# Moving two vector operations of each expert behind later weight splits in a mixture-of-experts kernel

## The chip, the cores and the metric

The kernel runs on one core of a Trainium2 chip. The figure is the device time of one execution in microseconds (us). TensorE (PE) multiplies matrices, VectorE (DVE) and ScalarE (ACT) work element by element, GpSimd (POOL) issues the gathers and scatters, SyncE (SP) issues the loads. Each engine works through its own queue in order; an instruction that waits holds up everything behind it on that engine.

## The reference

The program is a chain of a gated-linear-attention layer, a mixture-of-experts layer, a Fourier and attention layer and a recurrent layer on 512 tokens of width 1024. The change lies in the mixture of experts: 32 experts, each token goes to four of them.

```python
def expert_block(args):
    xblk, e = args
    gu = xblk @ w_gu[e] + b_gu[e]              # 1024 x 2048
    gate, up = jnp.split(gu, 2, axis=-1)
    gate = jnp.minimum(gate, SWIGLU_LIMIT)
    up = jnp.clip(up, -SWIGLU_LIMIT, SWIGLU_LIMIT)
    act = (up + 1.0) * gate * jax.nn.sigmoid(SWIGLU_ALPHA * gate)
    return act @ w_down[e] + b_down[e]         # 1024 x 1024
...
y = jnp.zeros((n_tok + 1, D_MODEL), yb.dtype).at[buf_tok].add(yb * buf_w[:, None].astype(yb.dtype))
```

## The kernel before

Every float32 product is made of three matmuls on rounded halves: a high part `hi` (a rounded copy, made by ACT, line 147) and a low part `lo` (source minus `hi`, made by DVE, line 148). Making the pair is called a split here. `W.get` loads one 1 MB block of weights (128 x 2048 values, tile `raw`, nine buffers) and splits it into `whi` and `wlo` (four pairs of buffers). So the split of a block can begin only when PE has finished with the block four before it, and SP may load a block only when the split nine before it is over.

One expert has twelve such blocks: eight of `w_gu` (called G0 to G7 here) and four of `w_down` (D0 to D3). Per pass of the loop over experts, the program's text has these steps: `gate_up(e)` (96 matmuls of 96 rows by 512 columns into `pgu`, four banks of PSUM, one buffer, and four more for the bias), `swiglu(e)`, `down(e - 1)` (48 matmuls into `pd`, one buffer, behind two for the bias), then `turn` of expert e's activation. In the middle of `gate_up(e)` the gathered tokens of expert e + 1 are turned (`pxT`, `xTh`, `xTl`), and in every fourth expert up to the 25th index tables for later experts are made (`tables`: matmuls `ptab` and small DVE operations).

The names on the path, in both programs:

- `g` and `u`: DVE reads `pgu` twice (lines 1166 and 1168 before), ACT applies Silu to `g` (L1167), DVE makes `u` of both (L1169). `pgu` is free for the next expert once the two reads are over.
- `paT`, `aTh`, `aTl`: PE turns `u` (L1128), ACT and DVE split it (L1134, L1135). `aTh`/`aTl` have one buffer, which the matmuls of `down` read.
- `y`: DVE scales `pd` (L1186) when `down` is over; POOL scatters it into the result (L1187).

What stands where on an engine is decided by a scheduler that reorders the instructions of the text by a model of their costs, unless an edge is given by hand. `tc.issue_after(ins)` gives such edges: each instruction in the block is placed behind `ins` on `ins`'s engine and waits for nothing more.

Of the kernel before, what the change touches and what calls it, by code (L numbers as in the profile page):

```python
# [9 lines left out]
F32 = mybir.dt.float32  # L10
# [5 lines left out]
OP = mybir.AluOpType  # L16
# [4 lines left out]
D = 1024  # L21
# [5 lines left out]
NE = 32  # L27
TK, XK, BK = 1, 5, 4

AH, SH, HN = 9, 7, 3  # L30
# [112 lines left out]
def split(S, hi, lo, src):  # L143
    if S.any:
        S.nc.any.tensor_copy(hi, src)
    else:
        S.nc.scalar.copy(hi, src)  # L147
    S.nc.vector.tensor_tensor(lo, src, hi.bitcast(F32), op=OP.subtract)  # L148


def mm3(S, ps, lh, ll, rh, rl, start, stop):
# [6 lines left out]
class Weights:  # L158
# [45 lines left out]
    def get(self, view, shape):  # L204
        S = self.S
        rv = self.early.pop(0) if self.early else self.load(view, shape)
        n = int(np.prod(shape[1:]))
        hi, lo = self.pair()
        hv, lv = hi[:shape[0], :n], lo[:shape[0], :n]
        if len(shape) == 3:  # L210
            hv = hv.rearrange("p (a b) -> p a b", a=shape[1])
            lv = lv.rearrange("p (a b) -> p a b", a=shape[1])
        split(S, hv, lv, rv)
        return hv, lv
# [742 lines left out]
def tables(S, pl, bank, b):  # L957

    nc = S.nc
    es = slice(b * 4, b * 4 + 4)  # L960
    oh = pl.tile([128, NT, 4, SLOTS], BF, name="oh", tag="oh", bufs=1)
    iota = S.k[:, None, K_IOTA:K_IOTA + SLOTS].to_broadcast([128, 4, SLOTS])
    for i in range(NT):
        nc.vector.tensor_tensor(oh[:, i], iota, S.pos[:, i, es, None].to_broadcast([128, 4, SLOTS]), op=OP.is_equal)
    p = bank("ptab")
    for e in range(4):
        for i in range(NT):
            nc.tensor.matmul(p[:SLOTS, e * 6:e * 6 + 6], oh[:, i, e, :], S.V[:, i, b * 4 + e, :], start=i == 0, stop=i == NT - 1)
    sl = pl.tile([SLOTS, 4, 6], F32, name="sl", tag="sl", bufs=2)
    nc.vector.tensor_copy(sl, p[:SLOTS, 0:24].rearrange("p (e c) -> p e c", e=4))  # L970
    t = pl.tile([SLOTS, 4, 4], F32, name="tsl", tag="tsl", bufs=2)
    tok, sct = t[:, :, 0], t[:, :, 1]
    nc.vector.tensor_tensor(tok, sl[:, :, 0], sl[:, :, 1], op=OP.add)
    nc.vector.tensor_copy(S.gi[:, es], tok)

    nc.vector.scalar_tensor_tensor(sct, sl[:, :, 2], S.k[:SLOTS, K_NSLOT:K_NSLOT + 1], tok, op0=OP.mult, op1=OP.add)
    nc.vector.tensor_scalar(S.si[:, es], sct, S.k[:SLOTS, K_SLOT:K_SLOT + 1], None, op0=OP.add)
    nc.vector.tensor_tensor(sct, sl[:, :, 3], sl[:, :, 4], op=OP.add)
    nc.vector.tensor_tensor(S.wt[:, es], sct, sl[:, :, 5], op=OP.add)
# [114 lines left out]
def phase_b(S):  # L1094
    nc, tc, I = S.nc, S.tc, S.I
    mm = nc.tensor.matmul
    with ExitStack() as bx:
# [4 lines left out]
        W = Weights(S, bx, 2048, 9, "b_w", (2, 3, 0, 1, 4, 5, 8, 6, 7))  # L1102
# [11 lines left out]
        xg, xT, aT, ac = {}, {}, {}, {}  # L1114

        def gather(e, gi=None):
            xg[e] = pl.tile([SLOTS, D], F32, name="xg", tag="xg", bufs=2)
            gi = S.gi[:, e:e + 1] if gi is None else gi
            S.gathered = nc.gpsimd.indirect_dma_start(out=xg[e], out_offset=None, in_=S.h2d,
                                         in_offset=bass.IndirectOffsetOnAxis(ap=gi, axis=0)).ins  # L1120

        def turn(src, dst, e, name, bufs, scale=1.0):
            dst[e] = [pl.tile([128, KT, SLOTS], F32R, name=name + n, tag=name + n, bufs=bufs) for n in "hl"]
            for h in range(2):
                p = bank("p" + name)
                for k in range(4):
                    kk = h * 4 + k
                    nc.tensor.transpose(p[:, k * SLOTS:(k + 1) * SLOTS], src[:, kk * 128:(kk + 1) * 128], S.ident[:SLOTS, :SLOTS])  # L1128
                hi, lo = [t[:, h * 4:h * 4 + 4, :] for t in dst[e]]
                p = p[:, :4 * SLOTS].rearrange("p (k t) -> p k t", k=4)  # L1130
                if scale == 1.0:
                    split(S, hi, lo, p)
                else:
                    nc.scalar.mul(hi, p, scale)  # L1134
                    nc.vector.scalar_tensor_tensor(lo, p, scale, hi.bitcast(F32), op0=OP.mult, op1=OP.subtract)  # L1135

        def bias(p, e, c, b, start, stop):
            lhs = sel[:, b // 3, e:e + 1].to_broadcast([128, SLOTS])
            mm(p[:, c * 512:(c + 1) * 512], lhs, bt[:, b % 3 * 512:(b % 3 + 1) * 512], start=start, stop=stop)  # L1139
# [7 lines left out]
        def gate_up(e, between):  # L1147
            p = ps.tile([SLOTS, 2048], F32, name="pgu", tag="gu", bufs=1)
            xh, xl = xT.pop(e)
            for k in range(KT):  # L1150
                if k in between:
                    between[k]()
                wh, wl = held.pop(0) if held else W.get(I["w_gu"][0, e, k * 128:(k + 1) * 128, :], [128, 2048])
                for a, w in ((xh, wh), (xh, wl), (xl, wh)):
                    for c in range(4):
                        mm(p[:, c * 512:(c + 1) * 512], a[:, k, :], w[:, c * 512:(c + 1) * 512],  # L1156
                           start=k == 0 and w is wh and a is xh, stop=False)
            for c in range(4):
                bias(p, e, c, c, False, True)
            return p  # L1160

        def swiglu(e, p):

            g = pl.tile([SLOTS, D], F32, name="g", tag="g", bufs=1)
            u = pl.tile([SLOTS, D], F32, name="u", tag="u", bufs=1)
            nc.vector.tensor_scalar(g, p[:, 0:D], 7.0, None, op0=OP.min)  # L1166
            nc.scalar.activation(g, g, AF.Silu, scale=ALPHA)  # L1167
            nc.vector.tensor_scalar(u, p[:, D:2 * D], 7.0, -7.0, op0=OP.min, op1=OP.max)  # L1168
            nc.vector.scalar_tensor_tensor(u, u, 1.0, g, op0=OP.add, op1=OP.mult)  # L1169
            return u  # L1170

        def down(e):
            p = ps.tile([SLOTS, D], F32, name="pd", tag="dn", bufs=1)
            for c in range(2):
                bias(p, e, c, 4 + c, True, False)
            ah, al = aT.pop(e)
            for k0 in range(0, KT, 2):
                wh, wl = W.get(I["w_down"][0, e, k0 * 128:(k0 + 2) * 128, :].rearrange("(k p) c -> p k c", p=128),
                               [128, 2, D])
                for k in range(2):  # L1180
                    for a, w in ((ah, wh), (ah, wl), (al, wh)):
                        for c in range(2):
                            mm(p[:, c * 512:(c + 1) * 512], a[:, k0 + k, :], w[:, k, c * 512:(c + 1) * 512],  # L1183
                               start=False, stop=k0 + k == KT - 1 and a is al)
            y = pl.tile([SLOTS, D], F32, name="y", tag="y", bufs=2)
            nc.vector.scalar_tensor_tensor(y, p, S.wt[:, e:e + 1], S.g2b, op0=OP.mult, op1=OP.mult)  # L1186
            nc.gpsimd.indirect_dma_start(out=S.ydr, out_offset=bass.IndirectOffsetOnAxis(ap=S.si[:, e:e + 1], axis=0),  # L1187
                                         in_=y, in_offset=None, compute_op=OP.add)

# [20 lines left out]
        held = [W.get(I["w_gu"][0, 0, k * 128:(k + 1) * 128, :], [128, 2048]) for k in range(HN)]  # L1210
# [3 lines left out]
        for e in range(NE + 1):  # L1214
            if e < NE:
                between = {BK: biases} if e == 0 else {}
                if e % 4 == 0 and e // 4 + 1 < NE // 4:
                    between[TK] = lambda: tables(S, pl, bank, e // 4 + 1)
                if e + 1 < NE:
                    between[XK] = lambda: turn(xg.pop(e + 1), xT, e + 1, "xT", 2)  # L1220
                p = gate_up(e, between)
                ac[e] = swiglu(e, p)
                if e == 6:
                    vectors(S, pl, bank)
                if e + 2 < NE:
                    gather(e + 2)
            if e > 0:
                down(e - 1)
            if e < NE:
                turn(ac.pop(e), aT, e, "aT", 1, 1.0 / ALPHA)  # L1230

# [712 lines left out]
```

## Time and profile before

| | us |
|---|---|
| runs (3) | 2264.12, 2265.87, 2269.25; median 2265.87 |
| profiled execution | 2268.54 |
| its span, first to last instruction | 2266.8 |
| PE busy | 2152.4 (95%) |
| DVE busy | 1807.6 (80%) |
| ACT busy | 1333.3 (59%) |
| mean granted TensorE clock | 0.981 |

An engine is busy while it runs an instruction; matmuls overlap, and their ends are modelled, so the distance between the starts of two groups of matmuls tells more than a matmul's duration. "Idle before <-X" is the time in which the engine stood still before an instruction, and X is what it waited for. The experts' stage is the stretch from some 316 to 1515 us.

### The profile page before, as it was taken

Reading aid. Unit: us, or ns where it says so; the run is one execution under the profiler, and the core shown is the slowest. Engines: PE = TensorE matmul, PEld = TensorE weight load, DVE = VectorE, ACT = ScalarE, POOL = GpSimd, SP = SyncE. Lnnn points to the kernel's source line nnn. Section 1 sums busy time; section 2 is a strip of 40 time slices with the busy share of each in tenths; the row PEclk is TensorE's granted clock in tenths of the full one; section 3 lists DMA queues with packets and bytes.
Section 4 is the critical chain, followed back from the end, with each engine's and each line's share of the span. In section 5 each row is a group of like instructions: output and inputs, shape, how many; then the busy total and the mean of one; then the engine's idle time right before and its main releaser. Section 6 shows DMA issues by size and latency. Waiting matters only on the chain.

```text
span 2266.8 us, 27655 instructions
## 1 busy us (share of the span) xinstructions
PE 2152.4 (95%) x10495; PEld 1627.5 (72%) x10495; DVE 1807.6 (80%) x2020; ACT 1333.3 (59%) x1489; POOL 301.3 (13%) x157
## 2 busy tenths in 40 slices
PE   6899979999999999999999999998999999999998
PEld 4787756777766666666666666667777888877876
DVE  5669789999988989898989898976478354689885
ACT  4335356777766666666666666754455443388862
POOL 1101120010122222222222121231000000000000
PEclk9899989999999999999999999999999999999999
DMA  7664579999999999999999999966311233423222
GB/s 269 196 218 151 190 253 338 378 366 368 363 344 353 357 358 354 356 353 364 345 359 351 363 355 365 337 199 223 103 47 47 84 121 131 129 66 93 93 84 93
DMA packets 155999, 561.96 MB, mean 248 GB/s; under 512 B 12964, under 2 KB 55304, under 8 KB 123080
## 3 DMA queue, kind: packets, MB, share of 16 engines
q1 hardware_dynamic: 144832, 522.37, 62.7%
q0 software_dynamic: 9968, 36.10, 6.0%
q10 hardware_dynamic: 1064, 1.70, 0.2%
q8 instruction: 83, 1.36, 0.2%
q14 instruction: 52, 0.43, 0.1%
HBM read 534.94 MB, written 25.58 MB: 247 GB/s over the span
## 4 chain that ended last, share of the span: by engine, by line
PE 81%; DVE 10%; DMA 4%; issue 3%; ACT 2%; POOL 1%; ACTq 0%; POOLq 0%; DVEq 0%; SPq 0%
PE pgu L1156 30%; PE pd L1183 12%; DVE wlo L148 3%; PE pjf L153 3%; PE pjf L154 3%; PE pjf L155 3%; PE pop L155 2%; PE pop L153 2%; PE pop L154 2%; DVE u L1168 1%; PE pgu L1139 1%; DMA ydr<-y,si 1%; DMA raw<-in_w_ada_dram 1%; PE pxT L1128 1%; PE paT L1128 1%
## 5 line engine op out<-in xcount | busy, mean ns | idle before, releaser
L148 DVE TENSOR_TENSOR wlo<-raw,whi 128x2048 fp32r<-128x2048 f32 (+2 forms) x498 | 1001.8, 2038 | 106.1 <-ACT whi L147 83.6
L147 ACT CAST whi<-raw 128x2048 fp32r<-128x2048 f32 (+2 forms) x454 | 790.6, 1777 | 191.6 <-PE pgu L1156 87.2
L1187 POOL DMA_INDIRECT ydr<-y,si x32 | 185.1, 5783 | 809.5 <-DVE y L1186 778.0
L1156 PE MATMUL pgu<-whi,xTh 128*96 128x512 f32 x1024 | 281.6, 396 | 2.6 <-DVE u L1168 2.6
L1156 PE MATMUL pgu<-wlo,xTh 128*96 128x512 f32 x1024 | 278.7, 394 | 0.3 <-DVE wlo L148 0.3
L1156 PE MATMUL pgu<-whi,xTl 128*96 128x512 f32 x1024 | 278.5, 394 | 0.0
L1156 PEld LDWEIGHTS pgu<-wlo,xTh 128*96 128x96 f32 x1024 | 165.5, 162 | 70.9 <-DVE wlo L148 0.7
L1156 PEld LDWEIGHTS pgu<-whi,xTl 128*96 128x96 f32 x1024 | 165.4, 162 | 69.8 <-issue 0.2
L1156 PEld LDWEIGHTS pgu<-whi,xTh 128*96 128x96 f32 x1024 | 161.7, 162 | 69.9 <-issue 3.0
L1183 PE MATMUL pd<-wlo,aTh 128*96 128x512 f32 x512 | 162.4, 398 | 32.5 <-DVE wlo L148 32.5
L153 PE MATMUL pjf<-xTh,whi 128*128 128x512 f32 (+1 forms) x480 | 181.8, 379 | 1.5 <-DVE rsq L221 1.5
L155 PE MATMUL pjf<-xTh,wlo 128*128 128x512 f32 (+1 forms) x480 | 180.5, 377 | 1.9 <-DVE wlo L148 1.9
L154 PE MATMUL pjf<-xTl,whi 128*128 128x512 f32 (+1 forms) x480 | 181.0, 377 | 0.0
L1183 PE MATMUL pd<-whi,aTh 128*96 128x512 f32 x512 | 159.7, 393 | 0.0
L1183 PE MATMUL pd<-whi,aTl 128*96 128x512 f32 x512 | 159.4, 392 | 0.0
L1183 PEld LDWEIGHTS pd<-wlo,aTh 128*96 128x96 f32 x512 | 79.1, 162 | 72.3 <-DVE wlo L148 43.2
L1167 ACT ACTIVATE g<-g 96x1024 f32<-96x1024 f32 x32 | 33.9, 1061 | 137.2 <-DVE g L1166 137.2
L1183 PEld LDWEIGHTS pd<-whi,aTh 128*96 128x96 f32 x512 | 82.4, 161 | 35.3
L1183 PEld LDWEIGHTS pd<-whi,aTl 128*96 128x96 f32 x512 | 82.4, 161 | 35.4
L155 PEld LDWEIGHTS pjf<-xTh,wlo 128*128 128x128 f32 x480 | 90.3, 188 | 18.7 <-DVE wlo L148 2.3
L153 PEld LDWEIGHTS pjf<-xTh,whi 128*128 128x128 f32 x480 | 90.5, 188 | 18.1 <-ACT jkr L1509 1.4
L154 PEld LDWEIGHTS pjf<-xTl,whi 128*128 128x128 f32 x480 | 90.5, 188 | 15.8
(536 smaller groups left out, 3511.7 us busy)
## 6 DMA issues: line engine op xcount, KB each, us to landing
raw<-in_w_gu_dram SPq DMA_DIRECT2D x254, 1024.0 KB, 9.6
raw<-in_w_down_dram SPq DMA_DIRECT2D x128, 1024.0 KB, 7.2
raw<-in_w_ada_dram SPq DMA_DIRECT2D x40, 512.0 KB, 5.6
raw<-in_even_w_in_dram SPq DMA_DIRECT2D x36, 512.0 KB, 3.4
raw<-in_odd_w_in_dram SPq DMA_DIRECT2D x32, 512.0 KB, 3.8
raw<-in_even_w_out_dram SPq DMA_DIRECT2D x16, 512.0 KB, 3.1
raw<-in_odd_w_out_dram SPq DMA_DIRECT2D x16, 512.0 KB, 3.2
raw<-in_w_in_dram SPq DMA_DIRECT2D x14, 512.0 KB, 3.7
```

The lines of the kernel that those rows point to most:

```text
L147: S.nc.scalar.copy(hi, src)
L148: S.nc.vector.tensor_tensor(lo, src, hi.bitcast(F32), op=OP.subtract)
L153: mm(ps, lh, rh, start=start, stop=False)
L154: mm(ps, lh, rl, start=False, stop=False)
L155: mm(ps, ll, rh, start=False, stop=stop)
L1128: nc.tensor.transpose(p[:, k * SLOTS:(k + 1) * SLOTS], src[:, kk * 128:(kk + 1) * 128], S.ident[:SLOTS, :SLOTS])
L1139: mm(p[:, c * 512:(c + 1) * 512], lhs, bt[:, b % 3 * 512:(b % 3 + 1) * 512], start=start, stop=stop)
L1156: mm(p[:, c * 512:(c + 1) * 512], a[:, k, :], w[:, c * 512:(c + 1) * 512], start=k == 0 and w is wh and a is xh, stop=False)
L1167: nc.scalar.activation(g, g, AF.Silu, scale=ALPHA)
L1168: nc.vector.tensor_scalar(u, p[:, D:2 * D], 7.0, -7.0, op0=OP.min, op1=OP.max)
L1183: mm(p[:, c * 512:(c + 1) * 512], a[:, k0 + k, :], w[:, k, c * 512:(c + 1) * 512], start=False, stop=k0 + k == KT - 1 and a is al)
L1187: nc.gpsimd.indirect_dma_start(out=S.ydr, out_offset=bass.IndirectOffsetOnAxis(ap=S.si[:, e:e + 1], axis=0), in_=y, in_offset=None, comput ...
```

## The change

The splits of D0, D1 and D2 of expert e - 1 are now taken in the text ahead of `swiglu(e)`, and `g`, `u` and the product `u` get an edge behind the last of them on DVE. At the end of `down(e - 1)` the splits of G0, G1 and G2 of expert e + 1 are taken (they are kept in `held`), and `y` gets an edge behind the last of these. The order of the loads on SP stays 8 blocks of `w_gu`, 4 of `w_down`, and so on.

```diff
-    S.nc.vector.tensor_tensor(lo, src, hi.bitcast(F32), op=OP.subtract)
+    S.split_last = S.nc.vector.tensor_tensor(lo, src, hi.bitcast(F32), op=OP.subtract).ins
...
-        def down(e):
+        def down_weights(e, k0):
+            return W.get(I["w_down"][0, e, k0 * 128:(k0 + 2) * 128, :].rearrange("(k p) c -> p k c", p=128), [128, 2, D])
+
+        def down(e, early):
...
-                wh, wl = W.get(I["w_down"][0, e, k0 * 128:(k0 + 2) * 128, :].rearrange("(k p) c -> p k c", p=128),
-                               [128, 2, D])
+                wh, wl = early.pop(0) if early else down_weights(e, k0)
...
+            if e + 2 < NE:
+                held.extend(W.get(I["w_gu"][0, e + 2, k * 128:(k + 1) * 128, :], [128, 2048]) for k in range(HN))
             y = pl.tile([SLOTS, D], F32, name="y", tag="y", bufs=2)
-            nc.vector.scalar_tensor_tensor(y, p, S.wt[:, e:e + 1], S.g2b, op0=OP.mult, op1=OP.mult)
+            with tc.issue_after(S.split_last):
+                nc.vector.scalar_tensor_tensor(y, p, S.wt[:, e:e + 1], S.g2b, op0=OP.mult, op1=OP.mult)
...
-                ac[e] = swiglu(e, p)
+
+                early = [down_weights(e - 1, k0) for k0 in (0, 2, 4)] if e else []
+                with tc.issue_after(S.split_last):
+                    ac[e] = swiglu(e, p)
...
+            else:
+                early = []
             if e > 0:
-                down(e - 1)
+                down(e - 1, early)
```

**Where the order moves.** In experts 0 to 6 the scheduler had put the splits in this order already: there DVE's rows are the same in both programs. From expert 8 on they differ. Three places of expert 17 follow, which stand for experts 9 to 30.

DVE before, around the reads of `pgu` of expert 17: the first `wlo` row is D0, and behind the product `u` come D2, D3 and G0 of the next expert.

```order
L148 TENSOR_TENSOR wlo_7768<-raw_7765,whi_7767 128x2048
L1166 TENSOR_SCALAR g_7754<-pgu_7589 96x1024
L1168 TENSOR_SCALAR u_7755<-pgu_7589 96x1024
L148 TENSOR_TENSOR wlo_7786<-raw_7783,whi_7785 128x2048
L1169 SCALAR_TENSOR_TENSOR u_7755<-u_7755,g_7754 96x1024
L148 TENSOR_TENSOR wlo_7804<-raw_7801,whi_7803 128x2048
L148 TENSOR_TENSOR wlo_7822<-raw_7819,whi_7821 128x2048
L148 TENSOR_TENSOR wlo_7860<-raw_7857,whi_7859 128x2048
L1186 SCALAR_TENSOR_TENSOR y_7837<-pd_7762,wt_2681,g2b_2682 96x1024
L1135 SCALAR_TENSOR_TENSOR aTl_7841<-paT_7842,aTh_7840 128x384
L1135 SCALAR_TENSOR_TENSOR aTl_7841<-paT_7849,aTh_7840 128x384
L148 TENSOR_TENSOR wlo_7878<-raw_7875,whi_7877 128x2048
```

DVE in the changed kernel, the same place: the first three `wlo` rows are D0, D1 and D2, the next is D3, and then come G0, G1 and, behind one half of `aTl`, G2.

```order
L148 TENSOR_TENSOR wlo_7757<-raw_7754,whi_7756 128x2048
L148 TENSOR_TENSOR wlo_7763<-raw_7760,whi_7762 128x2048
L148 TENSOR_TENSOR wlo_7769<-raw_7766,whi_7768 128x2048
L1166 TENSOR_SCALAR g_7772<-pgu_7607 96x1024
L1168 TENSOR_SCALAR u_7773<-pgu_7607 96x1024
L148 TENSOR_TENSOR wlo_7822<-raw_7819,whi_7821 128x2048
L1169 SCALAR_TENSOR_TENSOR u_7773<-u_7773,g_7772 96x1024
L148 TENSOR_TENSOR wlo_7840<-raw_7837,whi_7839 128x2048
L148 TENSOR_TENSOR wlo_7846<-raw_7843,whi_7845 128x2048
L1135 SCALAR_TENSOR_TENSOR aTl_7859<-paT_7860,aTh_7858 128x384
L148 TENSOR_TENSOR wlo_7852<-raw_7849,whi_7851 128x2048
L1192 SCALAR_TENSOR_TENSOR y_7855<-pd_7780,wt_2681,g2b_2682 96x1024
```

D1 and D2 have moved ahead of `g`, and G1 and G2 ahead of `y`: two splits more on either side.

ACT before, at the turn of the activation (`aTh`): the casts ahead of it are G0 and G1, the one behind it is G2.

```order
L147 CAST whi_7859<-raw_7857 128x2048
L147 CAST whi_7877<-raw_7875 128x2048
L1134 ACTIVATE aTh_7840<-paT_7842 128x384
L1134 ACTIVATE aTh_7840<-paT_7849 128x384
L147 CAST whi_7895<-raw_7893 128x2048
L147 CAST xTh_7947<-pxT_7949 128x384
```

ACT in the changed kernel, the same place: again G0, G1, `aTh`, G2, and then G3 and G4 ahead of `xTh`.

```order
L147 CAST whi_7839<-raw_7837 128x2048
L147 CAST whi_7845<-raw_7843 128x2048
L1134 ACTIVATE aTh_7858<-paT_7860 128x384
L1134 ACTIVATE aTh_7858<-paT_7867 128x384
L147 CAST whi_7851<-raw_7849 128x2048
L147 CAST whi_7913<-raw_7911 128x2048
L147 CAST whi_7931<-raw_7929 128x2048
L147 CAST xTh_7947<-pxT_7949 128x384
```

G2's cast stands behind `aTh` in both; the next tokens (`xTh`) come two casts later.

PE before, in the third block of `down` of expert 16: seven of the eight turns of `u` stand inside it.

```order
L1183 MATMUL pd_7762<-whi_7803,aTh_7573 96x512 x2
L1128 MATMUL paT_7842<-cst_k_60,u_7755 128x96 x4
L1128 MATMUL paT_7849<-cst_k_60,u_7755 128x96 x3
L1183 MATMUL pd_7762<-wlo_7804,aTh_7573 96x512 x2
```

PE in the changed kernel, in the fourth block: three matmuls of G0 stand inside it, and the eight turns of `u` behind it.

```order
L1156 MATMUL pgu_7874<-whi_7839,xTh_7680 96x512 x3
L1185 MATMUL pd_7780<-wlo_7822,aTh_7591 96x512 x2
L1185 MATMUL pd_7780<-whi_7821,aTl_7592 96x512 x2
L1185 MATMUL pd_7780<-whi_7821,aTh_7591 96x512 x2
L1185 MATMUL pd_7780<-wlo_7822,aTh_7591 96x512 x2
L1185 MATMUL pd_7780<-whi_7821,aTl_7592 96x512 x2
L1128 MATMUL paT_7860<-cst_k_60,u_7773 128x96 x4
L1128 MATMUL paT_7867<-cst_k_60,u_7773 128x96 x4
L1156 MATMUL pgu_7874<-whi_7839,xTh_7680 96x512
```

The turns of `u` have moved behind the last matmul of `down`; the turns of the next tokens (`pxT`) have moved from G1 into G3, and the two bias matmuls of the next `pd`, which follow them, come apart in most experts.

## Rows read from the trace of the kernel before

**Rows 1.** The page's first part: busy time, share of the span, instructions.

```profile
PE 2152.4 (95%) x10495; PEld 1627.5 (72%) x10495; DVE 1807.6 (80%) x2020; ACT 1333.3 (59%) x1489; POOL 301.3 (13%) x157
```

**Rows 2.** Waits of PE, whole span: in total, times, longest.

```profile
PE pd L1183 <- DVE wlo L148: 32.5, 23, 1.4
```

**Rows 3.** Two stretches: busy time by engine, granted clock, DMA share, GB/s.

```profile
400.00:660.00 260.00, 260.00 (x1229) 184.82 (x1228) 244.46 (x193) 183.08 (x126) 31.36 (x15) 1.00 0.99 363
660.00:1488.00 828.00, 796.70 (x3710) 560.24 (x3709) 734.72 (x478) 546.09 (x372) 194.35 (x41) 1.00 0.97 356
```

**Rows 4.** Timeline of PE, one late expert: start, length, instruction, idle before.

```profile
810.77 1.08 PE L1139 MATMUL pgu<-bt,sel 128*96 128x512 f32 x4
811.69 0.62 PE L1183 MATMUL pd<-whi,aTh 128*96 128x512 f32 x2
...
814.45 0.63 PE L1183 MATMUL pd<-whi,aTh 128*96 128x512 f32 x2
816.50 0.71 PE L1183 MATMUL pd<-wlo,aTh 128*96 128x512 f32 x2 [1.41 <-DVE wlo L148]
...
835.41 1.07 PE L1156 MATMUL pgu<-wlo,xTh 128*96 128x512 f32 x4
...
848.23 1.09 PE L1139 MATMUL pgu<-bt,sel 128*96 128x512 f32 x4
```

**Rows 5.** Timeline of DVE, the same late expert.

```profile
811.89 1.22 DVE L1166 TENSOR_SCALAR g<-pgu 96x1024 f32<-96x1024 f32 x1 [3.39 <-PE pgu L1139]
...
814.16 2.28 DVE L148 TENSOR_TENSOR wlo<-raw,whi 128x2048 fp32r<-128x2048 f32 x1
816.36 1.21 DVE L1169 SCALAR_TENSOR_TENSOR u<-u,g 96x1024 f32<-96x1024 f32 x1
817.50 6.68 DVE L148 TENSOR_TENSOR wlo<-raw,whi 128x2048 fp32r<-128x2048 f32 x3
825.18 1.28 DVE L1186 SCALAR_TENSOR_TENSOR y<-pd,wt,g2b 96x1024 f32<-96x1024 f32 x1 [1.00 <-PE pd L1183]
826.38 1.01 DVE L1135 SCALAR_TENSOR_TENSOR aTl<-paT,aTh 128x384 fp32r<-128x384 f32 x2
...
832.18 2.27 DVE L148 TENSOR_TENSOR wlo<-raw,whi 128x2048 fp32r<-128x2048 f32 x1
```

**Rows 6.** Timeline of ACT, the same late expert.

```profile
824.72 1.04 ACT L1134 ACTIVATE aTh<-paT 128x384 fp32r<-128x384 f32 x2 [3.30 <-PE pd L1183]
825.66 1.91 ACT L147 CAST whi<-raw 128x2048 fp32r<-128x2048 f32 x1
```

**Rows 7.** Timeline of PE, one early expert.

```profile
515.01 1.08 PE L1139 MATMUL pgu<-bt,sel 128*96 128x512 f32 x4
...
527.46 0.82 PE L1128 MATMUL paT<-cst_k,u 96*128 96x96 f32 x8
528.07 1.15 PE L1156 MATMUL pgu<-whi,xTh 128*96 128x512 f32 x4
...
550.87 1.09 PE L1139 MATMUL pgu<-bt,sel 128*96 128x512 f32 x4
```

**Rows 8.** Timeline of DVE, the same early expert.

```profile
516.65 1.21 DVE L1166 TENSOR_SCALAR g<-pgu 96x1024 f32<-96x1024 f32 x1
```

**Rows 9.** Timeline of PE, an early expert that makes tables.

```profile
442.53 1.09 PE L1139 MATMUL pgu<-bt,sel 128*96 128x512 f32 x4
...
479.15 1.08 PE L1139 MATMUL pgu<-bt,sel 128*96 128x512 f32 x4
```

**Rows 10.** Timeline of PE, a late expert that makes tables.

```profile
734.92 1.08 PE L1139 MATMUL pgu<-bt,sel 128*96 128x512 f32 x4
...
773.31 1.08 PE L1139 MATMUL pgu<-bt,sel 128*96 128x512 f32 x4
```

**Rows 11.** DMA from 400 to 660 us, in 40 slices of 6.5 us.

```profile
GB/s 369 399 365 342 354 426 344 401 356 314 421 381 349 361 347 343 430 348 398 314 358 384 396 366 374 383 336 426 355 332 367 381 306 418 335 362 322 265 300 386
```

**Rows 12.** DMA issues from 660 to 1470 us: KB each, us to landing.

```profile
raw<-in_w_gu_dram SPq DMA_DIRECT2D x170, 1024.0 KB, 10.4
```

**Rows 13.** DMA issues from 400 to 640 us.

```profile
raw<-in_w_gu_dram SPq DMA_DIRECT2D x51, 1024.0 KB, 7.9
```

## The prediction

> **What bounds the kernel now.** First the busy shares: PE is at work for 95% of the span and DVE for 80% [rows 1], so the question is what PE waits for. Then PE's waits: the longest entry is the matmuls of `down` waiting for a low half of a weight block, 32.5 us in 23 waits, the longest 1.4 [rows 2]. Then where these lie: from 400 to 660 us PE is busy 260.00 of 260.00 us; from 660 to 1488 us it is busy 796.70 of 828.00 [rows 3]. Nearly all 23 waits are thus in the later experts and none in the earlier ones (experts 3 to 8), which do the same work. The granted clock is 1.00 (the 2.4 GHz level) in both stretches, so it plays no part.
>
> One late expert shows the mechanism. PE ends G7 and the bias of `pgu` and goes straight into `down`, at 811.69 us; DVE has been idle for 3.39 us with `g` at the head of its queue, which waits for that bias [rows 4, 5]. D1's split stands behind `g` and `u`, starts at 814.16 and ends at 816.44; PE wants its low half half a microsecond after 814.45 and gets it at 816.50 [rows 4, 5]. DVE idles first and is late afterwards. In an early expert, where two splits more are done ahead of `g`, DVE comes to `g` with no idle time before it, 1.6 us after PE's bias group has started (516.65 against 515.01), and nobody waits for D1 [rows 7, 8].
>
> **The change part by part.** The number of matmuls, splits and transfers stays; only the order on DVE, and through the scheduler on ACT and PE, is new.
>
> *The wait that goes.* The recorded wait of 1.41 us starts at a modelled end of a matmul, so I take periods instead, from one bias group of `pgu` to the next. Late: 848.23 - 810.77 = 37.46 us [rows 4]. Early: 550.87 - 515.01 = 35.86 us [rows 7]. Difference 1.60. This agrees with the starts at the wait: 816.50 - 814.45 = 2.05 us, where a pair of `pd` matmuls otherwise starts every 0.46 (six pairs from 811.69 to 814.45, [rows 4]), so 1.59 is lost. In experts with tables the periods are 38.39 and 36.62, difference 1.77 [rows 9, 10]. Of the 23 waits four fall in late experts that make tables (12, 16, 20 and 24). Sum: 19 x 1.60 + 4 x 1.77 = 37.5 us. The recorded waits alone are the lower end of it, 32.4.
>
> *What is late next.* I follow one expert with `down` starting at 0, with durations from start to start in [rows 4 to 6]: pair of `pd` matmuls 0.46, block of twelve matmuls (of `pd` or `pgu`) 2.75, split 2.2, `g` and `u` 1.14 each, product `u` 1.14, `y` 1.20, half of `aTl` 0.5; a cast is 1.91 long. D2's buffer comes free when G6 is through, at -3.7; cast and split follow at once or as soon as DVE is free, which is at about 1.8. Then `g` and `u` run to 4.1, D3's split to 6.4 (PE wants it at 9.4, since three matmuls of G0 now stand inside `down`), the product `u` to 7.5, G0 to 9.7 and G1 to 11.9. PE leaves `down` at 11.0 + 0.7 = 11.7, turns `u` in 0.6 (527.46 to 528.07, [rows 7]) and wants G0's low half at 12.7, G1's at 15.4: more than 3 us of room each. PE's reuse of `pgu` at 8.7 finds it free since 4.1.
>
> The narrow place comes now. `aTh` must wait for the end of `down` (it does so before too: 3.30 us, [rows 6]) and now also for the turns of `u`, which follow it; it ends at 13.0. G2's cast stands behind it on ACT and runs to 15.0, its split on DVE to 17.3; PE wants it at 18.2. Behind G2 on DVE stand `y`, half of `aTl` and G3, whose split ends at 21.2; PE wants it at 20.9, and at 21.8 with the turns of the next tokens and a bias, which now stand inside G3. So 0.9 and 0.6 us of room. Is 0.6 enough? Before, G2's cast stands behind `aTh` as well [rows 6], and G3's split ends at 834.45 for a matmul at 835.41 [rows 4, 5]: 0.96 us of room, in 22 experts without a wait of note. From G4 on the room grows by 2.75 - 2.21 = 0.54 per block, less 0.9 for `xTl`, and is above 2 us at D0. I price the narrow place at 0, hidden by PE's own work on G1 and G2; without that cover each 0.1 us costs 0.1 x 22 = 2.2 us. In experts with tables DVE has 3.3 us more to do, PE about 0.8, which the room at D0 to G0 absorbs.
>
> *Does DVE have the time?* From 660 to 1488 us it is busy 734.72 us for 22 experts, 33.4 each [rows 3]; at a period of 35.9 that is 93%, and from 400 to 660 us it was 94% busy (244.46 of 260) without a wait of PE. It does, if hardly more.
>
> *PE's new cuts.* `down` is cut by three matmuls of G0, and the pair of biases comes apart. Matmuls of 512 columns between matmuls of 512 columns cost nothing that the rows show; behind turns the next pair is 0.06 longer. I allow 0.06 x 23 = 1.5 us, between 0 and 2.3 (0.1 each). `y` ends some 6.5 us after `down` (before: 1.5); the bias of the next `pd`, which needs it gone, stands in G3, 9 us after, and the scatter on POOL has a whole period. The end of the stage keeps its order (`y` of expert 30 right behind its `down`, then both scatters), so it only comes earlier.
>
> *Transfers.* The later experts move 356 GB/s [rows 3], 295 MB in 828 us; in 792 us that would be 372. The early stretch kept up 363 on average, with slices of 420 and more [rows 3, 11], and a block landed 7.9 us after its issue there against 10.4 later [rows 12, 13]. Hence there is headroom, and I add 0. The Trainium skill has a rule against that: "DMA: Bandwidth & Descriptors", section "Specifications", puts HBM traffic of a core at about 358 GB/s, and the section "Bandwidth" adds that this binds loads from HBM when both cores of a pair stream, while one core alone was measured at 425. This trace, of one core, agrees with the second: slices of 426 and 430.
>
> Sum against the profiled execution: 2268.5 - 37.5 + 1.5 = 2232.5 us. That execution lies 2.7 above the median of the runs (2265.87), from which the same step gives 2229.9. I forecast 2231.
>
> **Rivals.**
>
> *A part of the wait returns at G2 or G3.* For it: 0.6 us of room is little, and the turns of `u`, which stood inside `down`, now lie between its end and `aTh`. Against it: the passing handoff before, with 0.96. If my count is 0.9 to 1.4 us short, 0.3 to 0.8 us per expert are left, 7 to 18 us: 2238 to 2249, say 2243.
>
> *Transfers bind.* If loads cannot go above 358 GB/s for a whole stage, the 295 MB of the later experts need 823 us, and the gain is 5: about 2261. For it: DMA is busy 97 to 99% of both stretches [rows 3]. Against it: 363 GB/s over 260 us, and shorter landing times there.
>
> *The order changes but PE waits as long as before,* at another block in the same expert. For it: DVE's total work is the same and its queue is still in order. Against it: the early experts run just this order ahead of `g` with no wait at all. It would give 2266.
>
> *Slower.* G2's cast behind `aTh` becomes the wait of every expert. Before, seven of the eight turns were done in the middle of `down`; now ACT can begin only behind them all. From the point where G2's split ends later than 18.2 + 1.6 = 19.8 us after the start of `down` (2.5 later than reckoned), more is lost than gained; at 2.1 us lost per expert, 23 x (2.1 - 1.6) = 11 us: 2277. Against it: the turns take only 0.6 us, and a wait on DVE or ACT of this kind ends in 0.1 us or less (816.44 to 816.50, [rows 4, 5]).
>
> **How the numbers follow.** Forecast 0.66 (its own range 2225 to 2238: 37.5 plus the two cuts, and the two base times), part of the wait back 0.17, transfers 0.08, unchanged 0.04, slower 0.05. A difference of 0.2%, some 4.5 us, is what runs of this kernel can tell from none. Faster: 0.66 + 0.17 and half of the transfers' case, which lies at that bound, 0.87. Same: 0.04 and the other half, 0.08. Slower 0.05. The range from 2225 to 2248 leaves out the last three cases and a tail of the second.
>
> **What would show it.** Right: no wait of `pd` for `wlo` in the experts past 660 us; periods of 35.8 to 36.0 us (36.6 to 36.8 with tables) up to the last expert; no idle time before `g` on DVE; an idle time of 1 to 2 us on DVE before G2's split, put down to ACT's cast; DMA near 370 GB/s in this stretch. The experts before 620 us and everything behind the stage keep their lengths. Wrong: waits of PE for `wlo` at the third or fourth block of `pgu` (the first rival, or the slower one if above 1.6 us); casts waiting for `raw` (the transfers); `g` still idle behind PE's bias (the order not as it stands).

## The result and the profile after

The changed kernel takes 2226.36 us (median of 4 runs, 2224.67 to 2228.85); the kernel before, run beside it, 2265.30. The ratio is 0.9826, with a 95% interval of 0.9809 to 0.9843. The forecast was 2231, its own range 2225 to 2238. By the medians the fall is 38.9 us, where the sum had 36.0.

The profiled execution has a span of 2225.4 us. Its busy times answer to [rows 1]; the work is the same, the span is 41.4 us shorter. (The two profiled executions, 2268.54 and 2228.85 us, differ by 39.7; the span, first to last instruction, is what the timelines divide.)

```profile
PE 2143.6 (96%) x10495; PEld 1625.4 (73%) x10495; DVE 1808.1 (81%) x2020; ACT 1331.9 (60%) x1489; POOL 290.6 (13%) x157
```

PE's waits between 400 and 1480 us follow (total, times, longest). The line of [rows 2] is gone; the two that are left belong to the end of the stage.

```profile
PE pG L153 <- ACT ws L147: 3.1, 1, 3.1
PE pd L1139 <- DVE y L1192: 0.7, 1, 0.7
```

The two stretches of [rows 3], the second cut at 1450 us, where this stage now ends (columns as there): PE is busy without a gap in both, and the transfers go at 372 GB/s where they went at 356.

```profile
400.00:660.00 260.00, 260.00 (x1229) 184.81 (x1228) 246.63 (x195) 184.64 (x126) 28.87 (x14) 1.00 0.99 364
660.00:1450.00 790.00, 790.00 (x3701) 560.98 (x3700) 732.78 (x478) 543.56 (x372) 185.12 (x41) 1.00 1.00 372
```

PE in one late expert, the timeline that answers to [rows 4]. The matmul that waited 1.41 us is the one at 807.80; it now starts 0.46 after its neighbour. The three matmuls of G0 inside `down` stand at 813.33, the eight turns of `u` at 816.33, and G2, G3 and G4 want their low halves at 822.73, 826.39 and 829.13.

```profile
803.65 1.08 PE L1139 MATMUL pgu<-bt,sel 128*96 128x512 f32 x4
804.57 0.63 PE L1185 MATMUL pd<-whi,aTh 128*96 128x512 f32 x2
...
807.34 0.63 PE L1185 MATMUL pd<-whi,aTh 128*96 128x512 f32 x2
807.80 0.62 PE L1185 MATMUL pd<-wlo,aTh 128*96 128x512 f32 x2
...
813.33 0.86 PE L1156 MATMUL pgu<-whi,xTh 128*96 128x512 f32 x3
...
816.33 0.82 PE L1128 MATMUL paT<-cst_k,u 96*128 96x96 f32 x8
...
822.73 1.09 PE L1156 MATMUL pgu<-wlo,xTh 128*96 128x512 f32 x4
...
825.50 0.82 PE L1128 MATMUL pxT<-cst_k,xg 96*128 96x96 f32 x8
826.11 0.45 PE L1139 MATMUL pd<-bt,sel 128*96 128x512 f32 x1
826.39 1.07 PE L1156 MATMUL pgu<-wlo,xTh 128*96 128x512 f32 x4
...
829.13 1.09 PE L1156 MATMUL pgu<-wlo,xTh 128*96 128x512 f32 x4
...
839.54 0.63 PE L1139 MATMUL pgu<-bt,sel 128*96 128x512 f32 x2
```

DVE in the same expert, as in [rows 5]: it comes to `g` straight out of three splits, with no idle time, and idles later, where nobody waits for it: 1.62 us before G2's split, for ACT's cast.

```profile
799.47 6.68 DVE L148 TENSOR_TENSOR wlo<-raw,whi 128x2048 fp32r<-128x2048 f32 x3
806.08 1.21 DVE L1166 TENSOR_SCALAR g<-pgu 96x1024 f32<-96x1024 f32 x1
...
819.56 2.29 DVE L148 TENSOR_TENSOR wlo<-raw,whi 128x2048 fp32r<-128x2048 f32 x1 [1.62 <-ACT whi L147]
821.77 1.27 DVE L1192 SCALAR_TENSOR_TENSOR y<-pd,wt,g2b 96x1024 f32<-96x1024 f32 x1
822.97 0.54 DVE L1135 SCALAR_TENSOR_TENSOR aTl<-paT,aTh 128x384 fp32r<-128x384 f32 x1
823.43 4.48 DVE L148 TENSOR_TENSOR wlo<-raw,whi 128x2048 fp32r<-128x2048 f32 x2
```

And ACT, as in [rows 6]: `aTh` waits for the turns, and G2's cast stands behind it.

```profile
816.86 0.87 ACT L1134 ACTIVATE aTh<-paT 128x384 fp32r<-128x384 f32 x2 [4.60 <-PE paT L1128]
817.62 5.52 ACT L147 CAST whi<-raw 128x2048 fp32r<-128x2048 f32 x3
```

From bias group to bias group the late experts take 35.89 to 35.90 us, those with tables 36.61 to 36.64 (here 839.54 - 803.65 = 35.89). The span divides at the first and the last of these groups, experts 0 and 31: 341.81 became 341.47 us (0.3 gained), 341.81 to 1487.91 became 341.47 to 1451.24 (36.3 gained), and from there to the end of the span 778.9 became 774.2 (4.7 gained).

### The profile page after: what moved, and what is told of

Same layout as the page of the kernel before. It is cut to its first block, busy times and chain, and to the rows that moved or that the text cites. A ratio compares the mean times of both kernels' runs of the same rounds, so it can differ in the third digit from the quotient of the medians.

```text
span 2225.4 us, 27613 instructions
## 1 busy us (share of the span) xinstructions
PE 2143.6 (96%) x10495; PEld 1625.4 (73%) x10495; DVE 1808.1 (81%) x2020; ACT 1331.9 (60%) x1489; POOL 290.6 (13%) x157
## 4 chain that ended last, share of the span: by engine, by line
PE 86%; DVE 7%; DMA 3%; issue 2%; ACT 2%; POOL 1%; ACTq 0%; POOLq 0%; DVEq 0%; SPq 0%
PE pgu L1156 31%; PE pd L1185 16%; PE pjf L154 3%; PE pjf L153 3%; PE pjf L155 3%; PE pop L155 3%; PE pop L153 3%; PE pop L154 3%; PE pgu L1139 1%; DMA raw<-in_w_ada_dram 1%; DVE wlo L148 1%; PE pxT L1128 1%; PE paT L1128 1%; PE pd L1139 1%; PE pjt L155 1%
## 5 line engine op out<-in xcount | busy, mean ns | idle before, releaser
L1193 POOL DMA_INDIRECT ydr<-y,si x32 | 168.2, 5256 | 808.3 <-DVE y L1192 785.7
L1185 PEld LDWEIGHTS pd<-wlo,aTh 128*96 128x96 f32 x512 | 82.7, 162 | 35.8
L1134 ACT ACTIVATE aTh<-paT 128x384 fp32r<-128x384 f32 x64 | 27.8, 486 | 106.4 <-PE paT L1128 106.4
```

## The experiments

In what follows "period" is the time from one bias group of `pgu` to the next in late experts without tables. Each ratio is against the kernel before, run on the same chip.

**The blocks ahead of `g` alone.** `y` and the first blocks stand as before the change.

```
-            if e + 2 < NE:
-                held.extend(W.get(I["w_gu"][0, e + 2, ...]) for k in range(HN))
-            with tc.issue_after(S.split_last):
-                nc.vector.scalar_tensor_tensor(y, p, ...)
+            nc.vector.scalar_tensor_tensor(y, p, ...)
```

> Only the three down-projection blocks ahead of g (D0, D1, D2); y and the first blocks of the next-but-one expert as before the change. Theory (all of the gain is D1's split out of the way of g and u): periods of the late experts within 0.2 us of the changed kernel's 35.89, so 2226 to 2233 us; G1's split now stands behind y and both halves of aTl and by the durations of the rows ends 16.4 us after the start of down, where PE wants it at 16.3, so a wait of 0.1 to 0.3 us may stand there. Rival (the part at y is needed too, because without it G1 or G2 becomes the wait): 1 us or more per expert at G1 or G2, 2248 us or more.

Measured: 2228.70 us, 0.9832 (0.9816 to 0.9848). Periods 35.78 to 35.93. The wait at G1 is there, but only in the four experts with tables, where DVE has more to do, and once near the end; PE's waits from 660 to 1450 us in all:

```profile
PE pgu L1156 <- DVE wlo L148: 1.8, 5, 0.4
```

The experts with tables take 37.15 to 37.51 us instead of 36.6. So this part has the gain. From the bias group of expert 1 to that of expert 31 this kernel takes 2.1 us more than the changed one; the part at `y` is worth no more than that here, which whole runs cannot tell apart.

**Two blocks ahead of `g`.** As the last, and the list of early blocks shorter by one:

```
-                early = [down_weights(e - 1, k0) for k0 in (0, 2, 4)] if e else []
+                early = [down_weights(e - 1, k0) for k0 in (0, 2)] if e else []
```

> Two blocks (D0, D1) ahead of g instead of three, nothing at y. Theory: only D1 was late; D2's split then runs from about 2.5 to 4.7 us after the start of down, PE wants it at 6.0, so no wait is left: 2226 to 2232 us, period about 35.9, and g on DVE is idle again for about 1 us. Rival (the wait only moves on by one block, to D2, because DVE has that much less done ahead): 1 us or more per expert at D2, 2248 us or more.

Measured: 2229.21 us, 0.9834 (0.9817 to 0.9850). Period 35.78 to 35.82; PE waits 0.3 us from 660 to 1450 us, and DVE stands idle ahead of `g` for 22.7 us in 18 times, which costs nothing (PE's waits, then DVE's):

```profile
PE pgu L1156 <- DVE wlo L148: 0.3, 1, 0.3
DVE g L1166 <- PE pgu L1139: 22.7, 18, 2.0
```

D1 was the only block that was late. From the bias group of expert 1 to that of expert 31 this kernel takes 0.4 us less than the changed one, so neither D2 nor the part at `y` is needed for the gain.

**The part at `y` alone.** No early blocks, `g` issued plainly:

```
-                early = [down_weights(e - 1, k0) for k0 in (0, 2, 4)] if e else []
-                with tc.issue_after(S.split_last):
-                    ac[e] = swiglu(e, p)
+                early = []
+                ac[e] = swiglu(e, p)
```

> Only the part at y: G0 to G2 of the next expert ahead of y on DVE, g and u again ahead of D1. Theory: D1 still ends about 4.8 us after the start of down and PE wants it at 3.2, so the wait of 1.6 us stays in every late expert: periods of 37.4 to 37.5 us, 2258 to 2268 us, no gain in the stage. Rival (the gain came from DVE's not standing idle before y and so being further ahead in the next expert): about 2226 us, no wait of pd for wlo.

Measured: 2280.07 us, 1.0055 (1.0038 to 1.0071): slower than before, which neither theory had. D1's wait stayed as the theory says, and a second one came, at G6 (PE timeline, one period):

```profile
817.00 0.70 PE L1185 MATMUL pd<-wlo,aTh 128*96 128x512 f32 x2 [1.41 <-DVE wlo L148]
...
844.95 1.17 PE L1156 MATMUL pgu<-wlo,xTh 128*96 128x512 f32 x4 [0.52 <-DVE wlo L148]
```

The period is 38.31 to 38.44. ACT's timeline of the same period shows where G6 comes from: in this order the turns of the next tokens come late and in pieces on PE, their casts `xTh` stand in ACT's queue and wait for them, and four weight casts stand behind:

```profile
835.32 0.48 ACT L147 CAST xTh<-pxT 128x384 fp32r<-128x384 f32 x1 [3.62 <-PE pxT L1128]
835.70 1.91 ACT L147 CAST whi<-raw 128x2048 fp32r<-128x2048 f32 x1
840.29 0.48 ACT L147 CAST xTh<-pxT 128x384 fp32r<-128x384 f32 x1 [2.68 <-PE pxT L1128]
840.66 7.33 ACT L147 CAST whi<-raw 128x2048 fp32r<-128x2048 f32 x4
```

**The text order without the two orders to issue.** The blocks are asked for where the change asks for them, but `g` and `y` are not tied behind a split:

```
-                with tc.issue_after(S.split_last):
-                    ac[e] = swiglu(e, p)
+                ac[e] = swiglu(e, p)
...
-            with tc.issue_after(S.split_last):
-                nc.vector.scalar_tensor_tensor(y, p, ...)
+            nc.vector.scalar_tensor_tensor(y, p, ...)
```

> The requests of the blocks stand in the text as in the changed kernel, but the two orders to issue g and y behind the last split are left out; the scheduler then sets g, D1, u on DVE (D1 between g and u) and G0, y, G1. Theory: D1's split starts after g alone, 1.3 us after the start of down instead of 2.5, ends at 3.6 and is wanted at 3.2; 0.4 to 0.5 us of the 1.6 stay per expert, 9 to 11 us over 23 experts: 2233 to 2240 us, period about 36.3. Rival (what is needed is only that one element-wise step less stands ahead of D1, so all is gained): 2226 us. Second rival (the orders do all the work): 2266 us.

Measured: 2254.11 us, 0.9939 (0.9923 to 0.9956), period 36.90 to 36.93: a third of the gain. The expectation missed by at least 14 us; it followed D1 only. PE waits twice per expert (same timeline view):

```profile
812.15 0.63 PE L1185 MATMUL pd<-whi,aTh 128*96 128x512 f32 x2
813.07 0.71 PE L1185 MATMUL pd<-wlo,aTh 128*96 128x512 f32 x2 [0.28 <-DVE wlo L148]
...
815.45 0.63 PE L1185 MATMUL pd<-whi,aTh 128*96 128x512 f32 x2
816.40 0.70 PE L1185 MATMUL pd<-wlo,aTh 128*96 128x512 f32 x2 [0.32 <-DVE wlo L148]
```

By starts D1 is late by 813.07 - 812.15 - 0.46 = 0.46 us, as expected. But then `u` and D2's split follow on DVE, 1.14 + 2.20 = 3.34 us, while PE takes 2.75 for a block: from D1's low half to D2's it is 816.40 - 813.07 = 3.33 us, so another 0.58. Together that is 1.04 of the 1.05 by which the period exceeds 35.86. Here each element-wise step ahead of a block cost its own length, less the room that was left.

**All four blocks ahead of `g`.**

```
-                early = [down_weights(e - 1, k0) for k0 in (0, 2, 4)] if e else []
+                early = [down_weights(e - 1, k0) for k0 in (0, 2, 4, 6)] if e else []
```

> All four down-projection blocks ahead of g (D3 too), the rest as in the changed kernel. Theory: g, u come 2.2 us later on DVE but PE needs their result only 11.8 us after the start of down; no wait is added: 2224 to 2230 us, no difference from the changed kernel. Rival (g and u late hold pgu or the turns of u): 0.5 us or more per late expert, 2238 us or more.

Measured: 2229.35 us, 0.9829 (0.9812 to 0.9845), period 35.88 to 35.90, and 36.18 to 36.19 in the four experts that follow one with tables. PE waits for nothing from 660 to 1450 us. As expected: two, three or four blocks give the same time within what the runs can tell.

**The narrow place, dosed.** `y` computed twice, then three times; this adds DVE time just ahead of G3, and of G4.

```
-                nc.vector.scalar_tensor_tensor(y, p, ...)
+                for _ in range(2):
+                    nc.vector.scalar_tensor_tensor(y, p, ...)
```

> The changed kernel with y computed twice: 1.2 us more on DVE right ahead of G3's split. Theory (the narrow place is as reckoned; in the changed kernel G3's split ends 0.7 us before PE wants it, G4's 1.2 before): G3 is 0.5 us late in each late expert without tables, period 36.4 instead of 35.89, 19 x 0.5 = 10 us, and 2.4 us at the stage's end, where y stands on the path twice: 2239 us (2235 to 2242). Rival (the room is larger than reckoned, or DVE makes it up): only the end's 2.4, 2229 us.

> The changed kernel with y computed three times, one of the two more ahead of G3, the other ahead of G4. Theory: G3 late by 0.5 and G4 by 2.4 - 1.2 = 1.2 us in all, period 37.1, 19 x 1.2 + some 4 in experts with tables = 23 to 27 us, and 4.8 at the stage's end: 2252 to 2258 us. Rival (room larger, or DVE makes it up): the end's 4.8 alone, 2231 us.

Measured: twice 2240.34 us, 0.9874 (0.9858 to 0.9890); three times 2266.19, 0.9997 (0.9988 to 1.0007). The first is the expected time, but made up otherwise: the period is 36.21 to 36.24, 0.33 us more instead of 0.5, the experts with tables lose nothing (one of the four 0.13), and from the last bias group to the end of the span it is 5.9 us more instead of 2.4. Of these, 1.6 lie long after the stage: from the first `pop` matmul to the first `pga` (two tiles of later layers) this run takes 139.4 us where the changed kernel takes 137.8, and 3.4 us at a granted clock of 0.51 (the 1.2 GHz level) lie there. The first run with spare loads below has the same, so it does not come from `y`. That the total came out as expected is luck in part. Its waits from 660 to 1450 us:

```profile
PE pgu L1156 <- DVE wlo L148: 3.6, 18, 0.8
```

With three the period is mostly 37.2 to 37.4 from expert 12 on and the experts with tables lose 1.3 too, more than expected; DVE is busy 760 of 790 us there (96%), so it has hardly any time to catch up. Both say that the room at G3 is below 1.2 us. Beyond it time is lost fast: 2.4 us per expert on DVE, 7% of its work, eat the whole gain, 28.5 us of it between the first and the last bias group and 7.1 behind.

**Transfers, dosed.** Three loads of 256 KB more per late expert, into a tile that nothing reads:

```
+        def spare(e, h):
+            dump = pl.tile([128, 512], F32, name="dump", tag="dump", bufs=1)
+            nc.sync.dma_start(dump, I["w_gu"][0, e, h * 128:(h + 1) * 128, 0:512])
...
+                if 9 <= e < 31 and k in (3, 7):
+                    spare(e, k)
...
+                if 9 <= e < 31 and k0 == 6:
+                    spare(e, 0)
```

> The changed kernel with three loads of 256 KB more per late expert (rows of weights into a tile that nothing reads), one after every four blocks: 0.79 MB more on some 13.35, 394 GB/s at the same period. Theory (transfers have headroom at 372 GB/s): 2224 to 2232 us, no casts waiting for raw, landing times up. Rival (transfers are at their limit already): 0.79 MB by 372 GB/s is 2.1 us per late expert, 22 x 2.1 = 46 us: about 2272, period 38.0. In between (a limit between 372 and 394) a part of it.

Measured: 2251.67 us, 0.9925 (0.9908 to 0.9941), and yet the period is 35.81 at 391 GB/s. The loss lies ahead of the stage: the first bias group is at 366.89 us instead of 341.47. The first spare load had been put early into SP's queue, where it waited for its tile and the weight loads waited behind it (SP's waits from 100 to 400 us):

```profile
SPq L1149 <- PE pcnt L953: 63.3, 1, 63.3
```

So each spare load was tied behind the weight load ahead of it, in the second run of the pair with four instead of three per expert:

```
-            nc.sync.dma_start(dump, ...)
+            with tc.issue_after(W.last):
+                nc.sync.dma_start(dump, ...)
```

> As the run with three spare loads of 256 KB per late expert, with each spare load tied behind the weight load ahead of it, so that none stands early in the queue (there the first of them held the weight loads for some 25 us before the stage). Theory (transfers have headroom at 372 GB/s): the period stays at 35.8 to 35.9 at some 391 GB/s and the whole at 2224 to 2230 us. Rival (the spare loads cost by themselves): 2240 us or more.

> Four spare loads of 256 KB per late expert instead of three, tied in the same way: 1.05 MB more, 400 GB/s at the same period. Theory (headroom up to there): period 35.8 to 35.9, 2224 to 2231 us, landing times of weights 14 to 16 us. Rival (the limit lies just above the 391 GB/s seen): 0.26 MB by 391 GB/s is 0.67 us per expert, 15 us: about 2241.

Measured with three: 2224.39 us, 0.9820 (0.9803 to 0.9836). The added 0.79 MB per expert cost nothing; PE is never idle in the stretch (its window, columns as above):

```profile
660.00:1450.00 790.00, 790.00 (x3706) 561.09 (x3705) 737.33 (x479) 545.17 (x372) 160.65 (x41) 1.00 1.02 393
```

A block of weights lands 12.6 us after its issue (median) where it took 9.1 in the changed kernel; no wait of PE came of it.

Measured with four: 2276.24 us, 1.0043 (1.0026 to 1.0059), casts wait for their blocks, and the rate is 372 GB/s again. This does not show a limit of the transfers: SP's waits in the stretch name the spare loads, which all go into one tile, so that each waits for the one before to land and the weights stand behind it.

```profile
SPq L1150 <- DMA dump<-in_w_gu_dram: 592.6, 81, 17.4
```

What the transfers can do above 393 GB/s stays open.

No version was made that beats the changed kernel by more than the runs can tell: the best, 2224.39 with the spare loads, is 2 us below the changed kernel's median, and the intervals of the two ratios overlap.

## Why the prediction was right, point by point

**The wait** went as reckoned, and for the reason given: D1's split behind `g` and `u`. The runs show it from three sides: moving D1 alone gives the gain, moving only the other part does not, and one element-wise step ahead of D1 and one ahead of D2 leave a loss of the size that their durations give. The choice of periods over recorded waits was needed: recorded 0.28 + 0.32 against 1.05 lost in one run, 0.2 (3.6 in 18) against 0.33 in another, 1.41 against 1.57 that the period fell by here.

**The narrow place** was reckoned at 0.9 us of room at G2 and 0.6 at G3. Measured: G2's split ends at 819.56 + 2.29 = 821.85 for a matmul at 822.73, 0.88; G3's at about 825.71 for 826.39, 0.68; G4's at 827.91 for 829.13, 1.22. The idle time on DVE before G2 was forecast at 1 to 2 us and is 1.62. The first rival and the slower one, which hang on these 0.6 us, did not come; the run with `y` twice shows that 1.2 us more on DVE would have brought the first, at 0.33 us per expert.

**DVE's load** is 93% (732.78 of 790), as forecast; `y` ends 6.5 us after `down` (823.04 against 816.49), as forecast.

**Transfers**: 372 GB/s as forecast, without a wait. The run with 393 shows headroom beyond; the second rival, 358 GB/s for the stage, is refuted. The Trainium skill's figure of 358 ("DMA: Bandwidth & Descriptors", section "Specifications") is by this trace not a limit for a core that streams alone; its section "Bandwidth" says as much.

**What was mis-sized.** The span fell by 41.4 us, the sum had 36.0. The prediction put everything ahead of the late experts and all of the end but its own wait at nothing. The 5.4 divide so:

- The late experts up to the 30th gained 0.6 more than the sum gives them. It took off 1.60 for each wait and gave back 1.5 in all, 0.066 each, for PE's new cuts (its 0.06 x 23 is 1.4); the period fell by 1.57. The cuts may well cost what they were priced at: in two kernels where the pair of biases of `pd` stays together (the blocks alone, the placed spare loads) the period is 35.8, and here it is 35.89. What was off is then the yardstick of 35.86, taken from early experts with another order on PE.
- The last period, from expert 30 to 31, fell from 37.62 to 35.15, by 2.47 instead of 1.53, which is 0.9 more. Before, a second wait, recorded as 0.25 us, stood at G1 of expert 31 (its low half started 0.87 after the two biases of `pd`, which otherwise take 0.5): some 0.4. From there on PE's groups of four started every 0.93 us, where they start every 0.92 in the changed kernel: some 0.3. Why they did was not followed.
- The end, from the last bias group on, fell by 4.7 instead of the 1.5 of its own wait of `pd` less the cuts, which is 3.2 more; 0.6 of this is PE's wait for `y` ahead of the last `pd` (1.3 before, 0.7 now). For some 2 us the scatters on POOL bear evidence.
- The stretch from the bias group of expert 0 to that of expert 9 gained 0.3, and another 0.3 lies ahead of it.

The scatters: of each of the next fences the first row is the scatter of expert 30, the second that of expert 31 (POOL's timeline). Before:

```profile
1503.90 8.53 POOL L1187 DMA_INDIRECT ydr<-y,si  x1 [18.10 <-DVE y L1186]
1521.39 1.40 POOL L1187 DMA_INDIRECT ydr<-y,si  x1 [8.96 <-DMA ydr<-y,si]
```

The changed kernel:

```profile
1465.00 1.40 POOL L1193 DMA_INDIRECT ydr<-y,si  x1 [8.04 <-DVE y L1192]
1478.14 2.14 POOL L1193 DMA_INDIRECT ydr<-y,si  x1 [11.74 <-DVE y L1192]
```

Two blocks ahead of `g`:

```profile
1463.14 8.54 POOL L1190 DMA_INDIRECT ydr<-y,si  x1 [13.93 <-DVE y L1189]
1480.55 1.40 POOL L1190 DMA_INDIRECT ydr<-y,si  x1 [8.87 <-DMA ydr<-y,si]
```

Where the first takes 8.5 us, the second cannot go out when its `y` is done (1476.0 in the last kernel) but waits for the first to land. From the last bias group to the end of the span it is 774.1 to 774.7 us in three kernels where the first takes 1.40 (the changed one, the blocks alone, the placed spare loads) and 776.1 and 777.0 in two with all waits gone where it takes 8.5 or more (four blocks, two blocks). The first run with spare loads looks like an exception, with 1.40 and 775.9, but there the difference comes later: the next layer's first matmuls (`pxn`) start 44.4 us after its last bias group, as early as in the other three (44.2 to 45.4; 47.6 and 48.0 in the two with a long scatter), and 1.6 us are lost long after, between the first `pop` and the first `pga` (139.4 us against 137.8), where this run has 3.4 us at the lower granted clock (0.51, the third figure from the end):

```profile
1826.30:1829.70 3.40, 3.40 (x9) 2.64 (x9) 3.31 (x6) 0.47 (x1) 0.00 (x0) 0.51 0.44 177
```

The kernel with two blocks, whose last bias group comes at 1448.81, 2.4 us earlier than the changed kernel's, takes 2.8 us more from there and so is not faster; 2.0 of the 2.4 lie before the bias group of expert 1. The change did not aim at the scatters; that part of the gain came by chance. What is left of the end was not followed further.

## What to carry to other kernels

Where the engine that is waited for was idle shortly before, as DVE was here, look first at the order of its queue and only then at its speed: look for the instruction at its head that waits, and put work that is already possible ahead of it. Count the loss by the period, not by the recorded waits, and follow the queue block by block until the room stops shrinking: one late block cured may leave the next one late. An edge added for one engine moves the others too, as the turns and casts of the tokens showed, so a part that looks harmless has to be tried alone.

## What the hardware showed that was not expected

The scatters on POOL are short or long, and most long ones end 1.3 us after the end of a split on DVE: all 25 above 2.5 us in the kernel before and 23 of 24 in the changed one. With `y` computed twice or three times many end 1.9 to 3.2 after. A scatter takes 1.4 us in some experts and 5.9 in most late experts of the changed kernel:

```profile
823.32 5.90 POOL L1193 DMA_INDIRECT ydr<-y,si  x1 [27.38 <-DVE y L1192]
```

This one ends 1.31 us after the last of the two splits that run beside it (829.22 against 827.91). In the kernel before, beside runs of three and of eight splits at the stage's end, the scatter takes 8.53 and 19.54 us and ends 1.27 and 1.28 after the last split (1512.43 against 1511.16 in the first). The one of 21.2 us in the changed kernel ends 3.4 us after its run. And with the same neighbours at the same distances (the splits 0.57 to 0.58 us after its start) some scatters take 1.4 us and some 6.4 or 8.5: at the stage's end 1.40 in the changed kernel, 8.53 before. So the splits beside it do not settle a scatter's length; what decides was not found.

The Trainium skill ("SBUF — State Buffer", section "SBUF: two separate sides") has DVE and GpSimd share a pair of ports that one instruction holds whole; it counts a DVE operation with two inputs in SBUF among these only against a GpSimd operation that reads SBUF, and gives the pair to whichever starts first. That the long scatters end with the splits, which read two operands from SBUF, would fit a pair that DVE holds; that these scatters started ahead of the splits does not fit the rule, and no run here tests the ports by themselves.

One core took 393 GB/s from its transfers for 790 us beside an uninterrupted PE, at a mean DMA share that the profile gives as 1.02.
